# Four edits around the retention core and the down projections of a two-layer trunk: later residual rows, mixed items, own background buffers, output rows on ScalarE

## The chip, the cores and the metric

The kernel runs on one core of one Trainium2 chip. The metric is the device time of one execution in microseconds (us). Engines are named as in the profile: PE (TensorE matmul), PEld (its weight load), DVE (VectorE), ACT (ScalarE), POOL (GpSimd), SP (SyncE, which issues most DMAs).

## The reference

Two layers over a sequence of 1024 rows of width 1024, all in float32. Layer 0 mixes with a gated delta net, layer 1 with retention; each layer then has a convolutional feed-forward part. What the change touches is this:

```python
for i in range(DEPTH):
    mod = (e @ ada_w[i] + ada_b[i])[:, None, :]
    sh1, sc1, g1, sh2, sc2, g2 = jnp.split(mod, 6, axis=-1)
    y = mixers[i % N_MIXERS](x * (1.0 + sc1) + sh1)
    x = layer_norm(DN_ALPHA * x + (1.0 + g1) * y, ln_g[i, 0], ln_b[i, 0])
    y = conv_ffn(x * (1.0 + sc2) + sh2, ffn_up[i], ...)
    x = layer_norm(DN_ALPHA * x + (1.0 + g2) * y, ln_g[i, 1], ln_b[i, 1])

def retention(h, w_in, w_out):          # 4 heads, dk 256, dv 512, chunks of 128
    q, k, v, gate = split(h @ w_in)
    q, k = rot(q), rot(k) * dk ** -0.5  # rotary embedding
    # per head and chunk: state (256 x 512), scores (128 x 128) with a decay mask
    o = intra + inter                   # 128 x 512 for each head and chunk
    o = _standardize(o, 1e-6) * silu(gate)
    return o @ w_out
```

`_standardize` subtracts the mean and divides by the standard deviation of each row of 512.

## The kernel before

Float32 products are made of three products of split operands: `split` (L88) makes a high part with ACT (L89) and the rest with DVE or POOL (L90), and each pair is multiplied three times. The stages follow one another on the one core: the start and the gated delta net (to about 660 us in the profile), its output projection, the up projection of layer 0 (to 1195), its down projection (to 1430), retention's queries, keys and gates (to 1765), the retention core together with the value projection (to 2140), retention's output projection, then the up projection (2297 to 2740) and the down projection of layer 1.

**Order.** The program is unrolled in Python. A scheduler orders each engine's instructions by simulated times, and buffers belong to tags: `tl(tag, ...)` takes one of `BUFS[tag]` buffers, and a tile waits until the oldest one is free. In the delta net and in the core, `run` interleaves generators ("streams") by a planner's clock: a stream that yields a number comes back after so many planned us, and of those ready the one with the smallest priority goes first. The order of PE's matmuls there is fixed by `pq` (L642). The planned waits of the core are in `RL` (L1823): for instance `"b": 3.21` between the normalisation of a chunk's output and its transposes.

**Background work.** `bg` is a list of small units, and `bg_step` (L119) runs at fixed places: it finishes the pending unit and starts the next, so that a unit's data is loaded one step ahead. `bg_ada` makes the modulation vectors from `ada_w` (512 KB a unit, eight units a vector; L214 loads, L221 and L223 multiply and add on DVE). `bg_tag` names the buffers: "lane" within a Strassen stage, otherwise "wr", of which there are two and which also hold the raw weights of `load_w`. When head 2 of the core starts, `bg_ada(1, 2, "row")` adds eight units. `bg_gain` scales rows of the layer's input on POOL for later.

**Strassen stages.** `strassen` runs a list of items, each a pair of 128-column weight blocks, by seven products of half-size blocks (`wino`, L1216). The first two items go another way (`side`). PSUM results are copied by ACT (L1224), combined by DVE (L1154, L1213) and handed to the item's `sink`. In layer 1 the items are gates (`gate_item`: SiLU on ACT at L1667, then stored) and ropes (`rope_item`: for each half of the rows six DVE operations, L1651 to L1656, then stored; one item each for the query and key of a head). They come as two gates, eight ropes, six gates.

**Down projection.** `proj_gen` (L1274) makes seven products, p = 0 to 6, of `nj` = 11 steps each with `gate=None`: each step loads a left and a right block, splits them (`ops`, L1322), and does twelve matmuls. The results become the residual sum and the layer norm of two row halves (`finish`, `norm`). The residual of half 1 needs x scaled by the norm's gain and bias; `gain_half(n)` does this for 128 rows by 512 columns: load, two POOL operations (L1345), store from POOL's queue (L1346). It is called at steps 0, 2, 4 and 6 of p = 0 and 1. Half 0 is loaded at p = 2 and scaled on DVE (L1353), and half 1 is loaded at p = 5 (`xload`, L1348).

**Core.** For each head and chunk, `core` (L1728) makes the new state (`sc<-vv,kz`, two banks of tag `sc`, of which there are two), prepares the next chunk (`ret_front`: scores, transposed key `kz`), makes the output `po` in another `sc` bank (`sc<-vv,sThl` and, in float32, `sc<-Sr,qk`) and starts `ret_back`. That one takes the statistics from PSUM (L1774), normalises on DVE (L1780) into `on`, and after RL["b"] transposes `on` on PE (`mm<-cst,on`), multiplies by the gate (L1789) and stores the blocks, with four sums on POOL from chunk 4 on (L1811).

## Time and profile before

| what | value |
|---|---|
| median of 3 runs | 2973.52 us (2968.97 to 2977.79) |
| span of the profiled execution, first to last instruction | 2967.8 us |
| mean granted TensorE clock | 0.985 |
| PE / DVE / ACT / POOL busy, share of the span | 95% / 76% / 44% / 16% |
| DMA | 451.01 MB, mean 152 GB/s |

The profiled execution's own time is known by its span alone; the times of the runs hold some us more than a span, for what lies before the first and after the last instruction. Busy times are shares of the whole span, so a stage must be read by itself. Rows of the groups give line, engine, operation, output and inputs, count, then busy us and mean ns, then the idle time of the engine before them with what ended it. Rows of the waits give who waited for whom: us in total, times, longest. Rows of the stretches give start and end, length, busy us (count) of PE, PEld, DVE, ACT and POOL, the granted clock, the DMA share and GB/s. Rows of the timeline give start, length, engine, line and operation. Rows of one line's or one tile's instructions give minimum, median and maximum in ns.

### The profile page before, as it was taken

The numbers are of one execution on the slowest core, as the hardware profiler recorded it, in microseconds if no ns is written. First come the engines' busy times: TensorE is split into PE (matmuls) and PEld (weight loads), VectorE is DVE, ScalarE is ACT, GpSimd is POOL, SyncE is SP. The second block draws the span as 40 slices with busy tenths as digits, with TensorE's granted clock in tenths as the row PEclk, the third lists the DMA queues.
The fourth block names the chain that finished last, engine by engine and source line by source line (L and its number), as shares of the span: only waits on it lengthen the run. The fifth ranks groups of instructions, "written<-read, shape, count | busy, mean of one in ns | idle before, by whom it ended". The sixth has DMA issues, their size and how long they took to land. (4 is left out here: it accounts for less than half of the span.)

```text
span 2967.8 us, 38939 instructions
## 1 busy us (share of the span) xinstructions
PE 2820.5 (95%) x13638; PEld 2304.5 (78%) x13638; DVE 2242.4 (76%) x4005; ACT 1316.5 (44%) x2413; POOL 474.8 (16%) x469
## 2 busy tenths in 40 slices
PE   8999898999999999999999999999999999999997
PEld 7887777887788888787877887777777788887786
DVE  5787787656688888879678645666689887777979
ACT  4744564444544444446433442222344544444443
POOL 0312221100001111610000202322202011112301
PEclk9999999999999999999999999999999999999998
DMA  7231222254245445865333544665664243335753
GB/s 275 79 113 65 86 79 79 83 167 160 91 158 163 158 151 174 305 198 179 120 128 117 181 160 152 203 189 175 205 212 157 91 135 107 107 107 176 274 183 137
DMA packets 244404, 451.01 MB, mean 152 GB/s; under 512 B 23088, under 2 KB 76592, under 8 KB 244208
## 3 DMA queue, kind: packets, MB, share of 16 engines
q1 hardware_dynamic: 213088, 401.07, 41.0%
q10 hardware_dynamic: 29760, 43.00, 4.0%
q0 software_dynamic: 1360, 4.46, 0.4%
q8 instruction: 107, 1.75, 0.3%
q14 instruction: 89, 0.73, 0.1%
HBM read 339.91 MB, written 108.53 MB: 151 GB/s over the span
## 5 line engine op out<-in xcount | busy, mean ns | idle before, releaser
L651 PE MATMUL acc<-hT,wh 128*128 128x512 f32 x960 | 299.3, 393 | 0.0
L1437 PE MATMUL acc<-bb,ab 128*128 128x512 f32 x984 | 231.4, 393 | 6.6 <-DVE bb L90 5.4
L1585 POOL TENSOR_TENSOR o<-o 128x512 f32<-128x512 f32 x80 | 110.7, 1394 | 716.4 <-DVE o L1578 490.8
L1437 PEld LDWEIGHTS acc<-bb,ab 128*128 128x128 f32 x984 | 182.6, 188 | 50.2 <-DVE bb L90 10.2
L1163 PE MATMUL acc<-T,wb 128*128 128x512 f32 x840 | 203.1, 391 | 6.7 <-DVE wb L90 6.7
L651 PEld LDWEIGHTS acc<-hT,wh 128*128 128x128 f32 x960 | 181.9, 190 | 34.1
L651 PE MATMUL acc<-hT,wl 128*128 128x512 f32 x480 | 201.1, 419 | 0.0
L89 ACT ACTIVATE ab<-ar 128x512 fp32r<-128x512 f32 x210 | 129.6, 625 | 152.7 <-PE mm L287 36.9
L90 DVE TENSOR_TENSOR ab<-ar,ab 128x512 fp32r<-128x512 f32 x210 | 161.9, 777 | 41.1 <-ACT ab L89 41.1
L1163 PEld LDWEIGHTS acc<-T,wb 128*128 128x128 f32 x840 | 157.0, 188 | 43.2 <-DVE wb L90 9.8
L90 DVE TENSOR_TENSOR wl<-wr,wh 128x1024 fp32r<-128x1024 f32 x95 | 119.7, 1260 | 69.6 <-ACT wh L89 68.6
L90 DVE TENSOR_TENSOR wb<-mm,wb 128x512 fp32r<-128x512 f32 x216 | 145.5, 682 | 31.2 <-ACT wb L89 30.6
L90 DVE TENSOR_TENSOR wb<-wr,wb 128x512 fp32r<-128x512 f32 x162 | 111.1, 691 | 69.8 <-ACT wb L89 69.1
L89 ACT ACTIVATE wh<-wr 128x1024 fp32r<-128x1024 f32 x95 | 100.7, 1061 | 132.3 <-PE acc L651 53.1
L1224 ACT ACTIVATE pc<-acc 128x512 f32<-128x512 f32 x143 | 84.9, 593 | 160.7 <-PE acc L1163 97.4
L1564 DVE SCALAR_TENSOR_TENSOR o<-g,vc,o 128x512 f32<-128x512 f32 (+2 forms) x176 | 145.4, 843 | 4.7 <-ACT o L1559 4.1
L89 ACT ACTIVATE wb<-mm 128x512 fp32r<-128x512 f32 x216 | 124.0, 595 | 51.9 <-DVE mm L1213 50.3
L89 ACT ACTIVATE wb<-wr 128x512 fp32r<-128x512 f32 x162 | 99.4, 628 | 104.0 <-DMA wr<-in_ffn_up 38.8
L651 PE MATMUL acc<-wh,hT 128*128 128x512 f32 x384 | 135.6, 415 | 1.6 <-DVE vv L90 1.6
L110 PE MATMUL acc<-T,wb 128*128 128x512 f32 x292 | 116.0, 397 | 9.4 <-DVE wb L90 9.4
L472 DVE SCALAR_TENSOR_TENSOR qkv<-raw,vc,qkv 128x512 f32<-128x512 f32 x144 | 111.6, 779 | 11.5 <-ACT qkv L470 10.7
L223 DVE SCALAR_TENSOR_TENSOR ada<-mvw,e,ada 128x512 f32<-128x512 f32 x140 | 106.9, 764 | 17.4 <-DMA mvw<-in_ada_w 17.1
(641 smaller groups left out, 7466.8 us busy)
## 6 DMA issues: line engine op xcount, KB each, us to landing
wr<-in_ffn_up SPq DMA_DIRECT2D x92, 512.0 KB, 4.4
mvw<-in_ada_w SPq DMA_DIRECT2D x80, 512.0 KB, 4.3
ad<-o SPq DMA_DIRECT2D x154, 256.0 KB, 3.1
ar<-ad SPq DMA_DIRECT2D x154, 256.0 KB, 3.9
Br<-in_ffn_down SPq DMA_DIRECT2D x88, 256.0 KB, 3.8
wr<-in_ret_wv SPq DMA_DIRECT2D x32, 512.0 KB, 3.9
ar<-od SPq DMA_DIRECT2D x56, 256.0 KB, 5.3
xs<-xt ACTq DMA_DIRECT2D x24, 512.0 KB, 3.7
```

Of the source, the lines that this page charges most:

```text
L89: act.activation(dst_h, src, AF.Copy)
L90: eng.tensor_tensor(dst_l, src, dst_h, ALU.subtract)
L110: mm(acc, wl[:, k], hl[0], start=first, stop=False)
L223: dve.scalar_tensor_tensor(a, wr[:, kk], e[:, k:k + 1], a, ALU.mult, ALU.add)
L472: dve.scalar_tensor_tensor(oh, raw[:, 3 - j:515 - j], w[:, 3 - j:4 - j], oh, ALU.mult, ALU.add)
L651: pq(pe.matmul(out, lhsT, rhs, start=start, stop=stop), cost)
L1163: return pe.matmul(*a, skip_group_check=True, **kw)
L1224: act.activation(t, X, AF.Copy)
L1437: return pe.matmul(*args, skip_group_check=True, **kw)
L1564: dve.scalar_tensor_tensor(tv, gv[:, c0 - j:c1 - j], w[:, 2 - j:3 - j], tv, ALU.mult, ALU.add)
L1585: (dve if fp == 0 else pool).tensor_tensor(o[d], o[x], o[y], op)
```

## The change

- The row scaling of half 1 (`gain_half`) is called in p = 3 and 4 instead of p = 0 and 1, and its tile comes from the tag "xT" instead of "lane".
- The tag "xT" has two buffers instead of four; with the tiles that it now holds each is 4 KB a partition instead of 2.
- `bg_step` counts down: a unit returns a number of steps with its work. That is 2 where `bg_tag` is "xT", else 1. During the core `bg_tag` is "xT". The accumulator tile is taken when the work is done and not when the load is issued.
- After the first two gates, the order of items is rope, then three times rope and gate, rope, then three times rope and gate.
- `ret_back` copies `po` from PSUM with ACT, takes the statistics from the copy, makes minus mean times inverse deviation (one DVE and one POOL operation on a column) and normalises the copy in place with ACT (Identity with scale and bias). RL["b"] is 6.5 instead of 3.21.

```diff
-            "wr": 2, "wh": 2, "wl": 2, "t2": 3, "sm": 14, "sm2": 6, "st": 8, "s8": 6, "S": 4, "qx": 3, "fs": 1, "xT": 4}
+            "wr": 2, "wh": 2, "wl": 2, "t2": 3, "sm": 14, "sm2": 6, "st": 8, "s8": 6, "S": 4, "qx": 3, "fs": 1, "xT": 2}
...
     def bg_step(tile=mm_tile):
         bg_ps[0] = tile
-        if pend:
-            pend.pop()()
+        for p in pend:
+            p[0] -= 1
+        while pend and (pend[0][0] <= 0 or not bg):
+            pend.pop(0)[1]()
+            if not bg:
+                break
         if bg:
             nxt = bg.pop(0)()
             if nxt:
-                pend.append(nxt)
+                pend.append(list(nxt))
...
         def unit(nh, kp):
+            wr = tl(bg_tag[0], [P, 2, HALF], name="mvw")
+            c0 = j * D + nh * HALF
+            sp.dma_start(wr, A["ada_w"][i, kp * 256:(kp + 1) * 256, c0:c0 + HALF].rearrange("(a p) n -> p a n", p=P))
+            return 2 if bg_tag[0] == "xT" else 1, lambda: work(nh, kp, wr)
+
+        def work(nh, kp, wr):
             if kp == 0:
                 box["a"] = tl("ada", [P, HALF])
             a = box["a"]
...
-            x = tl("lane", [P, HALF], name="xg")
+            x = tl("xT", [P, HALF], name="xg")
...
-                if gain and p < 2 and j % 2 == 0 and p * 4 + j // 2 < 8 and j < 8:
-                    gain_half(p * 4 + j // 2)
+                if gain and p in (3, 4) and j % 2 == 0 and j < 8:
+                    gain_half((p - 3) * 4 + j // 2)
...
-    B = strassen(h0, xts, sc_r, sh_r, [gate_item(0), gate_item(2)]
-                 + [rope_item(h, j) for h in range(RH) for j in range(2)] + [gate_item(u) for u in range(4, 16, 2)], ("hTa", "aux", "qkv", "qkv", "hTa"), True)
+    ropes = [rope_item(h, j) for h in range(RH) for j in range(2)]
+    gates_ = [gate_item(u) for u in range(4, 16, 2)]
+    mixed = [ropes.pop(0)] + [r for k in range(3) for r in (ropes.pop(0), gates_.pop(0))] + [ropes.pop(0)]
+    mixed += [r for k in range(3) for r in (ropes.pop(0), gates_.pop(0))]
+    B = strassen(h0, xts, sc_r, sh_r, [gate_item(0), gate_item(2)] + mixed, ("hTa", "aux", "qkv", "qkv", "hTa"), True)
...
     def ret_back(h, n, po):
+        on = tl("t2", [P, HALF], name="on")
+        act.activation(on, po, AF.Copy)
         st = tl("st", [P, 2, 6], name="rst")
-        dve.bn_stats(st[:, 0], po)
+        dve.bn_stats(st[:, 0], on)
         mv = tl("s8", [P, 4], name="mv")
         dve.bn_aggr(mv[:, 0:2], st[:, 0])
         dve.tensor_scalar(mv[:, 2:3], mv[:, 1:2], 1e-6, None, ALU.add)
+        dve.tensor_scalar(mv[:, 1:2], mv[:, 0:1], -1.0, None, ALU.mult)
         pool.tensor_tensor(mv[:, 3:4], mv[:, 2:3], mhalf[:, 0:1], ALU.pow)
-        on = tl("t2", [P, HALF], name="on")
-        dve.tensor_scalar(on, po, mv[:, 0:1], mv[:, 3:4], ALU.subtract, ALU.mult)
+        pool.tensor_tensor(mv[:, 0:1], mv[:, 1:2], mv[:, 3:4], ALU.mult)
+        act.activation(on, on, AF.Identity, bias=mv[:, 0:1], scale=mv[:, 3:4])
         yield RL["b"]
...
-    RL = {"v": 2.57, "q": 5.9, "f": 3.35, "p": 0.55, "c": 2.75, "b": 3.21, "o": 4.42}
+    RL = {"v": 2.57, "q": 5.9, "f": 3.35, "p": 0.55, "c": 2.75, "b": 6.5, "o": 4.42}
...
+    bg_tag[0] = "xT"
     run([(0.0, ret_fill())] + [(-1.0, core(h)) for h in range(RH)])
+    bg_tag[0] = "wr"
```

More of the change, by code (lines that the diff above doesn't have):

```diff
@@ L211, in unit @@
             a = box["a"]
-            wr = tl(bg_tag[0], [P, 2, HALF], name="mvw")
-            c0 = j * D + nh * HALF
-            sp.dma_start(wr, A["ada_w"][i, kp * 256:(kp + 1) * 256, c0:c0 + HALF].rearrange("(a p) n -> p a n", p=P))
-            return lambda: work(nh, kp, a, wr)
-        def work(nh, kp, a, wr):
             for kk in range(2):
@@ L389, in unit @@
                 return gain(x, rs, c)
-            return lambda: gain(x, rs, c)
+            return 1, lambda: gain(x, rs, c)
         def gain(x, rs, c):
```

## The prediction

> **What bounds the kernel now.** I read the page first, then the busy time of the engines in stretches that follow the stages, then the waits of PE in each stage, and last the timeline at single waits.
>
> ```profile
> span 2967.8 us, 38939 instructions
> PE 2820.5 (95%) x13638; PEld 2304.5 (78%) x13638; DVE 2242.4 (76%) x4005; ACT 1316.5 (44%) x2413; POOL 474.8 (16%) x469
> ```
>
> PE is the bound almost everywhere, so the change can win only the time in which PE stands still, 147 us at most, and of that only what lies in the stages that it touches. Those are the two down projections (1196 to 1430 and 2736 to 2968), the Strassen stage of the retention's q, k and gates (about 1481 to 1765) and the retention core (1765 to 2140).
>
> ```profile
> core 0: us, PE busy (x) PEld busy (x) DVE busy (x) ACT busy (x) POOL busy (x), PEclk, DMA share, GB/s
> 1196.00:1236.00 40.00, 33.00 (x137) 25.89 (x136) 33.83 (x40) 18.12 (x39) 31.98 (x18) 0.96 1.02 376
> 1236.00:1265.00 29.00, 29.00 (x129) 24.01 (x128) 28.98 (x39) 15.85 (x28) 21.29 (x9) 1.00 0.79 272
> 1326.00:1356.00 30.00, 30.00 (x134) 24.83 (x133) 24.65 (x41) 8.49 (x15) 0.00 (x0) 1.00 0.46 148
> 1356.00:1394.00 38.00, 36.18 (x168) 28.75 (x167) 36.46 (x71) 26.90 (x45) 3.60 (x4) 1.00 0.59 194
> 1765.00:2140.00 375.00, 350.97 (x1568) 269.45 (x1567) 232.24 (x419) 93.61 (x159) 96.67 (x113) 0.99 0.59 182
> 2829.00:2859.00 30.00, 30.00 (x134) 24.83 (x133) 18.84 (x30) 13.14 (x24) 0.00 (x0) 1.00 0.61 194
> 2859.00:2890.00 31.00, 31.00 (x139) 25.66 (x137) 30.63 (x52) 13.44 (x25) 0.00 (x0) 1.00 0.59 187
> 2890.00:2919.00 29.00, 29.00 (x129) 24.02 (x128) 29.00 (x56) 16.43 (x31) 4.37 (x3) 1.00 0.49 155
> 2919.00:2949.00 30.00, 29.51 (x128) 23.49 (x126) 26.80 (x51) 7.19 (x12) 5.43 (x3) 1.00 0.39 132
> ```
>
> A down projection is seven products of eleven steps, about 30 us each. The first two rows are products p = 0 and 1 of layer 0, rows three and four its p = 4 and 5; the last four rows are p = 3 to 6 of layer 1. Three things are to be seen. At the start (1196) PE misses 7 us of 40 while POOL is busy for 32 and the DMA engines are full. In the core PE misses 24 us of 375, and ACT is idle for three quarters. And in the last layer DVE has 11.2 us free in p = 3, but is full from 2859 on: there DVE, not PE, sets when the kernel ends.
>
> The waits of PE, by stage: 1196 to 1236, 2720 to 2800, 1481 to 1765, and the core.
>
> ```profile
> PE acc L285 <- DVE ab L90: 7.0, 4, 2.8
> ...
> PE acc L285 <- DVE ab L90: 4.9, 3, 2.6
> PE acc L286 <- DVE bb L90: 0.8, 2, 0.4
> ...
> PE acc L1163 <- DVE wb L90: 5.3, 5, 1.1
> PE sc L1163 <- DVE wb L90: 2.7, 3, 1.1
> ...
> PE sc L651 <- DVE on L1780: 8.0, 6, 2.5
> PE mm L654 <- DVE on L1780: 7.2, 4, 3.1
> PE sc L651 <- DVE Sr L1752: 3.5, 1, 3.5
> ...
> PE acc L651 <- DVE wl L90: 1.0, 2, 0.8
> ```
>
> These 40 us are all that can be reached: 12.7 at the starts of the two down projections, 8.0 in the Strassen stage, 19.7 in the core.
>
> **Later residual rows.** Eight times a layer, `gain_half` loads 256 KB, runs two POOL operations on it and stores it from POOL's queue. This leaves p = 0 and 1 and goes to p = 3 and 4, four in each. What POOL does to DVE is seen in the splits of the left operand, in 1196 to 1265 (first row) and in 2859 to 2965, where POOL hardly works (second); the third row is one POOL operation.
>
> ```profile
> L90 DVE TENSOR_TENSOR ab<-ar,ab 128x512 fp32r<-128x512 f32 x26 | 26.0, 1014 | 7.6 <-ACT ab L89 7.6
> ...
> L90 DVE TENSOR_TENSOR ab<-ar,ab 128x512 fp32r<-128x512 f32 x29 | 19.5, 677 | 0.0
> ...
> L1345 POOL TENSOR_TENSOR xg<-xg,rowb x32: 1257/1625/20702, 1199.6 to 2782.6; 128x512 f32<-128x512 f32 x32
> ```
>
> Beside POOL the split takes 1014 ns instead of 677: 26 x 0.337 = 8.8 us of DVE in that stretch from this group alone, with 27 POOL instructions beside it. At the start, where no operands are ahead yet, PE waits for just these splits. The four sums of the last feature pair (L1585) stay on POOL, and the first operands still have to land, so I let 2.0 of the 7.0 us stay in layer 0 and 1.7 of 5.7 in layer 1: -5.0 and -4.0.
>
> What it costs later: p = 3 hides its four rows (11.2 us of free DVE in layer 1; layer 0 runs the same products). In p = 4 there are eight POOL operations and four stores. Their price to DVE lies between 8.8 / 27 x 12 = 3.9 us and the full length of the operations, 8 x 1.257 = 10.1; I take 6, since the splits are only the largest of DVE's groups. In layer 0, p = 4 leaves DVE 5.35 us free and the next product 1.5, so 0.5 is left over. In layer 1 nothing covers it, and DVE's chain to the end grows: +6. DVE works in order, so the splits for the next steps and the residual sums of p = 4 queue behind a held operation, and PE waits for the splits. SP's queue gains the loads in p = 3 and 4 where the DMA share is 0.46 to 0.61, which I count as nothing; on a full queue, as at 1196, they would delay operand loads. The rows are read only in the half-1 loads of p = 5. Layer 0: -4.5 (-7 to +3). Layer 1: +2 (-5.7 to +6.1).
>
> The Trainium skill, SBUF — State Buffer (section "SBUF: two separate sides"), says that VectorE and GpSimd share one port pair as an exclusive lock: whichever starts first holds it for its whole instruction, and the other fully blocks. The longer splits agree in kind; by the whole-instruction price the upper end, 10.1, would hold, which speaks against the move into a full DVE.
>
> **The core's output rows.** In `ret_back` DVE reads `po` from PSUM, and its last reader is the normalisation (L1780), which waits for POOL's power (L1778). Groups of the core, one small DVE operation, and the nearest row to the new normalisation (ACT, Identity with bias and scale columns):
>
> ```profile
> L651 PE MATMUL sc<-Sr,qk 128*128 128x512 f32 x112 | 52.6, 592 | 0.0
> ...
> L1780 DVE TENSOR_SCALAR on<-sc,mv 128x512 f32<-128x512 f32 x32 | 25.9, 808 | 34.6 <-POOL mv L1778 34.6
> ...
> L89 ACT ACTIVATE vv<-acc 128x512 fp32r<-128x512 f32 x32 | 19.1, 596 | 37.3 <-PE acc L651 33.8 <-DVE mv L1777 2.4
> L1778 POOL TENSOR_TENSOR mv<-mv,mhalf 128x1 f32<-128x1 f32 x32 | 17.6, 551 | 135.0 <-DVE mv L1777 135.0
> ...
> L1811 POOL TENSOR_TENSOR ot<-ot,op 128x256 f32<-128x256 f32 x15 | 14.5, 967 | 1.9 <-DMA od<-ot 1.8
> ...
> 1898.86 0.15 DVE L1777 TENSOR_SCALAR mv<-mv 128x1 f32<-128x1 f32 x1
> ...
> L1376 ACT ACTIVATE xt<-xt,mv x8: 802/810/817, 2919.5 to 2961.8; 128x512 f32<-128x512 f32 x8
> ```
>
> After the change PSUM is free after one ACT copy, 0.6 us by the `vv` row, which waits for no POOL. The six waits of PE for the `sc` bank, 8.0 us, go. What is late next is the bank's own turn:
>
> ```profile
> 1894.42 0.47 ACT L1719 ACTIVATE kz<-mm,vc 128x256 fp32r<-128x256 f32 x1 [3.63 <-PE mm L654]
> ...
> 1892.70 0.50 PE L651 MATMUL sc<-vv,kz 128*128 128x512 f32 x1 [1.02 <-DVE on L1780]
> ...
> 1901.15 1.07 PE L651 MATMUL sc<-vv,kz 128*128 128x512 f32 x4
> ```
>
> A chunk's state matmuls (`sc<-vv,kz`) need `kz`, which ACT begins at 1894.42 and PE uses at 1901.15, 6.7 us later, so ACT can be late by some 5 us at no cost.
>
> The chain to the transposes of `on` grows: copy 0.60, negation 0.15, POOL product 0.55, with the normalisation equal (0.81 on both engines): +1.3 us. The planner's delay b goes from 3.21 to 6.5, which puts the transposes behind the next chunk's `po`, whose four state matmuls alone take 52.6 / 28 = 1.9 us. The slack grows by at least 0.6, so of the 7.2 us (four waits) I take off 3. Bounds: all of it, or 4 x 1.3 = 5.2 more. DVE loses 32 x 0.81 = 26 us of work and the 34.6 us in which it stood before L1780 with `Sr`, `kz` and `wl` queued behind; it isn't the bound here, so this counts nothing. ACT gains 32 x 1.41 = 45 us in a stage where it is idle for 281, and takes over the wait for POOL, with `kz`, `sThl`, `wh` and `vv` behind it. I charge 2 us for that (0 to the price of the third rival). Together -8 - 3 + 2 = -9.
>
> **Own background buffers.** The eight loads of `ada_w` in the core share the two `wr` buffers with the value weights, and DVE stands in order before their data:
>
> ```profile
> DVE ada L223 <- DMA mvw<-in_ada_w: 12.0, 5, 4.9
> ```
>
> With two `xT` buffers and a countdown of two steps, each work item comes a step later than now, and a step is about one chunk, 9 us, against the 4.9 waited at most. PE's two waits behind it (`Sr` 3.5, `wl` 1.0) should go: -4 (-4.5 to 0). SP issues the same loads. With a count of 1, as everywhere else, `bg_step` does what it did; at the start only two `xT` tiles are used.
>
> **Mixed items.** Each rope item adds twelve DVE operations, and PE waits once an item, 8.0 us over eight waits. The first row is in a rope item, the second in the first gate item after the last rope, as the ACT row (SiLU of a gate) shows:
>
> ```profile
> 1549.50 0.72 PE L1163 MATMUL acc<-T,wb 128*128 128x512 f32 x2 [1.06 <-DVE wb L90]
> ...
> 1651.51 0.73 PE L1163 MATMUL acc<-T,wb 128*128 128x512 f32 x2 [1.06 <-DVE wb L90]
> ...
> 1651.07 0.61 ACT L1667 ACTIVATE pc<-pc 128x512 f32<-128x512 f32 x1
> ```
>
> The wait is the same, 1.06 us. It belongs to the item that follows a rope, whatever that is: the rope's operations run into it. There are still eight such items, so I take 0 (-8.0 if the gates drain them, +4 if output DMAs and `cv` buffers of two kinds collide).
>
> **The sum.** -4.5 + 2 - 9 - 4 + 0 = -15.5 us. Against the profiled span that is 2952.3. The median of the runs, 2973.5, lies 5.7 above the span, launch and spread together; I carry that over: 2958.
>
> **The rivals.** First, mixing drains the burst: without the eight waits it is 2950. For it: DVE is less loaded in gate items; against it: the two rows above.
>
> Second, POOL holds DVE for the whole length of its operations: 10.1 instead of 6 in p = 4 of both layers. Layer 0 then has 10.1 - 5.35 = 4.7 left over instead of 0.5, layer 1 gets 10.1: +8.3, 2966. For it: DVE is at 100% from 2859; against it: POOL's 20.7 us maximum shows that DVE also holds off POOL. The Trainium skill's page SBUF — State Buffer, cited above, would give this one.
>
> Third, slower: ACT stands before the new normalisation until POOL has worked off its queue. POOL's sums (up to 1 us each, four together) and the remaining row gains already made DVE wait 34.6 us in 26 waits. It decides when ACT is late by more than the 5 us at `kz`, or the transposes by more than their 0.6 us. If then each of 32 chunks costs PE 1.5 us, as the ten waits of now do on average (15.2 / 10), that is 48 instead of 15.2: +33 and the other terms' -6.5, 3000. Against it: ACT's idle 75%.
>
> Fourth, nothing comes of the core: the released bank is not what PE needs, and the next wait (for `Sr` or a split) takes the place of the 11 us. Then 2969.
>
> **How the numbers follow.** The forecast has 0.50, with a range of its own of 2948 to 2966; mixing 0.13; the full hold 0.12; ACT 0.12; the core for nothing 0.13. A measurement here can tell about 0.3%, 8.9 us: faster is below 2964.6. That holds for most of the forecast (0.47), the mixing (0.13), and some of the full hold and the core (0.09): 0.69. The same: 0.03 + 0.16 = 0.19. Slower: 0.12. The range of 2938 to 2980 holds all but the third rival and the lower bounds of several terms at once.
>
> **What would show it.** Right: no PE wait on `on` for `sc` in the core, under 5 us for its transposes; no DVE wait for `mvw`; PE waits under 4.5 us at the starts of the down projections; rope waits of about 1.06, eight times; DVE's work after PE's last matmul some us longer. Wrong: ACT waiting for POOL with `kz` late; the last layer's p = 4 to 6 longer by over 8 us; no more waits after ropes.

## The result and the profile after

The changed kernel takes 2975.4 us (median of 20 runs, 2963.6 to 2983.4), the kernel before 2973.7 (20 runs): ratio 1.0004, 95% interval 0.9995 to 1.0014. Nothing that can be measured came of it. The time is inside the range of the prediction, but not the gain of 15.5 us. The profiled execution has 3.3 us more span than that of before. First the page of the changed kernel:

```profile
span 2971.1 us, 39084 instructions
...
PE 2821.3 (95%) x13638; PEld 2306.7 (78%) x13638; DVE 2220.4 (75%) x4005; ACT 1360.0 (46%) x2477; POOL 479.4 (16%) x501
```

PE does as many matmuls as before, so the two traces can be laid side by side by the time at which the k-th matmul begins. The difference, after minus before, at the edges of the stages, worked out from both traces (one execution of each kernel):

| from matmul to matmul (about, us) | difference goes from, to | change | forecast |
|---|---|---|---|
| start of layer 0's down projection (1145 to 1268) | -2.8 to -12.2 | -9.4 | -5 |
| its p = 2 to 6 (to 1496) | -12.2 to +6.7 | +18.9 | +0.5 |
| q, k and gates (to 1734) | +6.7 to +2.9 | -3.8 | 0 |
| passage into the core (to 1791) | +2.9 to +10.4 | +7.5 | none |
| core (to 2213) | +10.4 to +9.3 | -1.1 | -13 |
| layer 1's down projection (2568 to its last matmul, 2949) | +9.5 to +3.7 | -5.8 | +2 |

The rows moved from the start are worth more than forecast, in both layers. One place takes that back at once: p = 3 and 4 of layer 0. The stretches of the changed kernel, columns as in the prediction:

```profile
1196.00:1236.00 40.00, 40.00 (x179) 33.11 (x178) 31.96 (x52) 24.31 (x51) 20.14 (x4) 1.00 0.85 304
...
1326.00:1356.00 30.00, 23.25 (x96) 19.12 (x97) 26.42 (x44) 5.14 (x9) 0.00 (x0) 0.83 0.55 180
...
1765.00:2140.00 375.00, 355.46 (x1563) 272.57 (x1564) 205.14 (x407) 133.04 (x220) 108.58 (x145) 0.97 0.59 183
...
2859.00:2890.00 31.00, 30.11 (x133) 24.95 (x134) 30.28 (x51) 12.23 (x23) 0.00 (x0) 1.00 0.61 187
```

In the first row PE is busy for all of its 40 us, against 33.00 before. In the second it does 96 matmuls where 134 were done before, at a granted clock of 0.83: it stood, and then ran slowly for a while. The core does as many matmuls in 375 us as before (1563 against 1568), although DVE works 27 us less in it.

The waits of PE in the changed kernel, for 1310 to 1345, 1481 to 1750, 1750 to 1800 and the core:

```profile
PE sc L289 <- DVE u L1414: 16.5, 1, 16.5
...
PE acc L1167 <- DVE wb L90: 3.9, 5, 1.1
PE sc L1167 <- DVE wb L90: 1.6, 2, 1.0
...
PE acc L655 <- DVE vv L90: 1.7, 2, 0.9
PE acc L655 <- ACT wh L89: 1.1, 1, 1.1
PE mm L270 <- DMA xlo<-xs: 1.1, 1, 1.1
...
PE mm L658 <- ACT on L1790: 9.3, 4, 4.4
PE acc L655 <- DVE ab L90: 3.8, 1, 3.8
PE acc L655 <- DVE vv L90: 3.0, 5, 0.9
```

One wait of 16.5 us is new. The waits after ropes fell from 8.0 to 5.5, but at 1750 to 1800 `xlo`, `wh` and `wl` are waited for as well, where before there was one wait of 1.0 for `vv`. In the core the waits of `sc` on the output row are gone, as forecast, and those of its transposes are 9.3 instead of 7.2.

**The wait of 16.5 us, followed back.** DVE stood first; then what SP's queue did (waits of SP from 1270 to 1335, then its timeline):

```profile
DVE Br L1321 <- DMA Br<-in_ffn_down: 18.1, 3, 16.3
```

```profile
SPq L1347 <- DMA xg<-xg: 24.6, 4, 10.9
SPq L1636 <- POOL xg L1349: 7.7, 3, 4.2
...
SPq L215 <- DMA xg<-xg: 2.5, 2, 1.4
```

```profile
1309.17 0.44 SPq L1307 DMA_DIRECT2D Br<-in_ffn_down  x1
...
1317.07 0.33 SPq L1636 DMA_DIRECT2D trig<-in_trig  x1
1318.84 0.38 SPq L215 DMA_DIRECT2D mvw<-in_ada_w  x1
1319.32 0.42 SPq L1307 DMA_DIRECT2D Br<-in_ffn_down  x1
```

SP issues one load after the other. The load of a row (L1347) waits until one of the two `xT` buffers is free, that is until the store of the row two back has landed; the loads of the rotary tables (L1636) wait for buffers that the rows' gain and bias hold; the core's first background units (L215), which the scheduler has moved up to here, wait for the same two buffers. Behind all of them stand the operand loads. The block `Br` that DVE needs was issued at 1319.32 and DVE went on at 1324.49. PE's wait ends at 1332.75, at the first matmul of p = 4.

The rows were late for a reason of their own. POOL's first scaling, and DVE beside it:

```profile
1259.17 13.92 POOL L1349 TENSOR_TENSOR xg<-xg,rowb 128x512 f32<-128x512 f32 x2 [33.73 <-DMA xg<-xs]
...
1269.56 0.69 DVE L90 TENSOR_TENSOR ab<-ar,ab 128x512 fp32r<-128x512 f32 x1
1270.76 1.18 DVE L90 TENSOR_TENSOR ab<-ar,ab 128x512 fp32r<-128x512 f32 x1 [0.52 <-ACT ab L89]
1271.87 1.77 DVE L90 TENSOR_TENSOR bb<-Bw,bb 128x512 fp32r<-128x512 f32 x1
```

```profile
L1349 POOL TENSOR_TENSOR xg<-xg,rowb x16: 1262/1453/12222, 1259.2 to 1317.1; 128x512 f32<-128x512 f32 x16
```

The last row (minimum, median and maximum in ns) shows one of the first two operations at 12.2 us against a median of 1.45. DVE worked without a gap at 0.69 us an operation, and only after its first gap (0.52 us at 1270) did POOL come through and DVE's operations grow to 1.2 to 2.5 us. The two longest scalings of the kernel before (20.7 and 13.1 us) end the same way: all three are done some 1.15 us after DVE's first gap since their start begins.

The rows don't run where the prediction placed them either. They are called in the steps of p = 3 and 4, but operands are made about a product ahead of PE: in layer 0 POOL scales from 1259 to 1318, while PE is in p = 2 and 3 (from 1256 up to its wait), and in layer 1 from 2799 to 2852, again in p = 2 and 3 (2799 to 2860):

```profile
L1349 POOL TENSOR_TENSOR xg<-xg,rowb x16: 1286/1622/2487, 2799.1 to 2850.1; 128x512 f32<-128x512 f32 x16
```

### The profile page after: what moved, and what is told of

The parts are those of the page before. It is cut to its first block, busy times and chain, and to the rows that moved or that the text cites. A ratio compares the mean times of both kernels' runs of the same rounds, so it can differ in the third digit from the quotient of the medians.

```text
span 2971.1 us, 39084 instructions
## 1 busy us (share of the span) xinstructions
PE 2821.3 (95%) x13638; PEld 2306.7 (78%) x13638; DVE 2220.4 (75%) x4005; ACT 1360.0 (46%) x2477; POOL 479.4 (16%) x501
## 4 chain that ended last, share of the span: by engine, by line
PE 74%; DVE 11%; DMA 6%; ACT 5%; issue 3%; POOL 1%; SPq 0%; ACTq 0%; POOLq 0%; DVEq 0%
PE acc L655 15%; PE acc L1167 10%; PE acc L110 6%; PE acc L111 5%; PE acc L112 5%; PE sc L1167 5%; PE sc L655 4%; PE acc L1441 3%; PE mm L655 2%; PE sc L111 2%; PE sc L112 2%; PE sc L110 2%; DVE ab L90 1%; PE mm L658 1%; DVE bb L90 1%
## 5 line engine op out<-in xcount | busy, mean ns | idle before, releaser
L1589 POOL TENSOR_TENSOR o<-o 128x512 f32<-128x512 f32 x80 | 126.8, 1595 | 792.0 <-DVE o L1582 558.8
L1167 PE MATMUL acc<-T,wb 128*128 128x512 f32 x840 | 203.0, 390 | 5.0 <-DVE wb L90 5.0
L110 PE MATMUL acc<-T,wb 128*128 128x512 f32 x292 | 116.0, 397 | 9.4 <-DVE wb L90 9.4
L111 PE MATMUL acc<-T,wb 128*128 128x512 f32 x292 | 115.5, 396 | 0.0
```

Source lines behind the costliest of these rows:

```text
L110: mm(acc, wl[:, k], hl[0], start=first, stop=False)
L111: mm(acc, wh[:, k], hl[1], start=False, stop=False)
L1167: return pe.matmul(*a, skip_group_check=True, **kw)
L1589: (dve if fp == 0 else pool).tensor_tensor(o[d], o[x], o[y], op)
```

## The experiments

Times are medians; a ratio is to the kernel before, run on the same chip, with its 95% interval. The versions are named in bold. "C" is the changed kernel.

### The rows and SP's queue

**Rows back.** C with

```diff
-            x = tl("xT", [P, HALF], name="xg")
+            x = tl("lane", [P, HALF], name="xg")
...
-                if gain and p in (3, 4) and j % 2 == 0 and j < 8:
-                    gain_half((p - 3) * 4 + j // 2)
+                if gain and p < 2 and j % 2 == 0 and p * 4 + j // 2 < 8 and j < 8:
+                    gain_half(p * 4 + j // 2)
```

> The changed kernel with the row scaling back at steps 0 to 6 of p = 0 and 1, in the buffers of the lane; the rest stays changed. Theory (the row loads wait for buffers on SP's queue, and the operand loads of layer 0's p = 3 and 4 stand behind them): PE's single wait of 16.6 us for u is gone, and the starts of the two down projections lose their gains of 9.5 and 8.8 us again. Against the changed kernel -19.6 + 9.5 + 8.8 - 2.7 = -4 us, about 2971. Rival (the long wait comes from elsewhere, the other loads that were hoisted into p = 4): the 16.6 us stay and the starts are lost as well, 2993.

2973.3 us, 1.0004 (0.9993 to 1.0015). PE has no wait at all from 1270 to 1345. So the late rows bring the long wait, and as C has them they are worth nothing that can be told; the theory's -4 is within the uncertainty, the rival's 2993 is not.

**Rows from POOL's queue.** C with

```diff
             with after("w"):
-                sp.dma_start(x, gain[1][rs, hs(hf)])
+                pool.dma_start(x, gain[1][rs, hs(hf)])
```

> The changed kernel, with the eight row loads of each layer issued from POOL's queue instead of SP's; the POOL work and the place stay. Theory: the 24.6 us in which SP stood before row loads are gone, but four loads of the rotary tables stand in SP's queue ahead of the operand loads of p = 3 and wait for the buffers of the row vectors, which are held until the last row is done; so SP stands there once, for 5 to 20 us, and PE's wait in p = 3 or 4 falls only in part, to 5 to 12 us: 2965 to 2972. Rival (POOL takes DVE's port, and what is late is DVE's split): POOL does the same work and more issues, so the wait of 16.6 us stays, 2975.

2970.4 us, 0.9987 (0.9977 to 0.9996), and no wait of PE from 1270 to 1345. But this run doesn't answer its question: without SP's order to hold them, the scheduler moved the row loads to the start of the up projection (the units' loads of SP then stood 18.5 us there in the next version, and both lost nearly 8 us between the 4000th and the 5000th matmul, with one PE wait of 9.3 us for `wb` in the next version, 4.7 in C).

**The same, tables last.** Also

```diff
-                    sp.dma_start(t[hf], (A["trig"][i] if j else A["trigq"][h, i])[:, hs(hf)])
+                    with after("a"):
+                        sp.dma_start(t[hf], (A["trig"][i] if j else A["trigq"][h, i])[:, hs(hf)])
```

> As the one before, and the loads of the rotary tables are ordered behind the last left block of the down projection, so that no load of SP's queue waits for the row work. Theory: PE's wait in p = 3 and 4 is under 2 us, the loss of 19.6 us of that stretch is at most 3, against the changed kernel -16 to -19: 2957 to 2960, 0.5% below the kernel before. Rival (port): 16.6 us stay, 2975.

2967.9 us, 0.9983 (0.9973 to 0.9992). Against the kernel before, the profile stands at -4.1 after p = 1 and at -3.2 after p = 6: p = 2 to 6 cost 0.9 instead of 18.9. The total missed 2957 to 2960, since the place at the up projection cost nearly 8.

**Four buffers.** C with four buffers of 2 KB:

```diff
-            ... "fs": 1, "xT": 2}
+            ... "fs": 1, "xT": 4}
...
-    bg_tag[0] = "xT"
     run([(0.0, ret_fill())] + [(-1.0, core(h)) for h in range(RH)])
```

> The changed kernel with four buffers of 2 KB for the rows and the background units of the core back in the raw weights' buffers. Theory: each row's load waits for the store four rows back instead of two, so SP stands for under 8 us instead of 24.6, and the rotary tables' 7.7 us stay; PE's wait falls from 16.6 to 3 to 8 us, -9 to -14, and the core gets back DVE's wait for its unit (about +4 on PE, as before) but loses the 4.5 us stall of the transposes at 2044: 2961 to 2967. Rival (port): 2975.

2965.2 us, 0.9970 (0.9959 to 0.9982). The waits for row buffers are gone; what is left are the tables, as expected (PE, then SP):

```profile
PE sc L289 <- DVE u L1414: 6.6, 1, 6.6
```

```profile
SPq L1636 <- POOL xg L1349: 18.5, 4, 11.8
```

**Four buffers, tables last.** Both edits.

> The changed kernel with four row buffers of 2 KB, the core's background units back in the raw weights' buffers, and the rotary tables' loads ordered behind the last left block of the down projection: with the row loads still on SP, no load there waits for the row work for longer than the rows' own buffers make it. Theory (SP's queue): the 18.5 us in which SP stood for the tables in the version with four buffers alone are gone, PE's wait for u in layer 0's p = 4 (6.6 us there, 16.6 in the changed kernel) falls under 1.5, and the stretch p = 3 and 4 loses at most 2 us against the kernel before: -7 to -9 us against that version, 2956 to 2958. Rival (POOL and DVE share a port, the rest of 6.6 us is DVE's): as the version with four buffers, 2965.

2961.1 us, 0.9963 (0.9951 to 0.9975). No wait for row work is left in SP's queue, none on `u` in PE's; from matmul 6500 to 7500 the difference goes from -9.7 to -8.5. That settles it: POOL does the same row work in the same products, and without SP's waits the stretch costs 1.2 us. (POOL's first scaling took 8.6 us in this trace. In "Late rows and own buffers" below it took 12.3, as in C, and PE has no wait on `u` there either.) The price of the queue by itself is this version against C without own buffers (below, 2976.4 on the same chip, the same rows in two buffers): 15 us.

### One part of C undone

**Items as before.** C with

```diff
-    B = strassen(h0, xts, sc_r, sh_r, [gate_item(0), gate_item(2)] + mixed, ...
+    B = strassen(h0, xts, sc_r, sh_r, [gate_item(0), gate_item(2)]
+                 + [rope_item(h, j) for h in range(RH) for j in range(2)] + [gate_item(u) for u in range(4, 16, 2)], ...
```

> The changed kernel with the items in the order of before (two gates, eight ropes, six gates). Theory (mixing wins 3.5 us of waits after ropes and loses 7.5 us where the stage goes over into the core, since the last rope ends at 1747 instead of 1652 us and its stores, the loads of q and k and the first row scalings then fall on the first value weights): the loads of xlo land before they are needed again, no PE waits over 0.9 us from 1755 to 1800, and -4 us against the changed kernel, to -7 if the transposes' wait of 3.4 us at 1879 goes as well: 2968 to 2971. Rival (the loss at the stage's end belongs to the core's edit): the rope waits return and nothing else moves, +3.5, 2979.

2970.8 us, 0.9991 (0.9981 to 1.0001), 0.13% or 4 us better than C's 1.0004, as the theory has it, though the intervals overlap. In the profile the waits after ropes are back (5.8 and 3.2), the passage into the core costs 0.1 us instead of 7.5, and at 1750 to 1800 there is only this:

```profile
PE acc L655 <- DVE vv L90: 1.0, 1, 1.0
```

**Output rows on DVE as before.** C with the whole head of `ret_back`, and b, of before:

```diff
-        act.activation(on, po, AF.Copy)
-        dve.bn_stats(st[:, 0], on)
+        dve.bn_stats(st[:, 0], po)
...
-        pool.tensor_tensor(mv[:, 0:1], mv[:, 1:2], mv[:, 3:4], ALU.mult)
-        act.activation(on, on, AF.Identity, bias=mv[:, 0:1], scale=mv[:, 3:4])
+        dve.tensor_scalar(on, po, mv[:, 0:1], mv[:, 3:4], ALU.subtract, ALU.mult)
```

> The changed kernel with the output rows of the core on DVE as before, with the delay b of 3.21. Theory (the 8.0 us of PE waits for sc are gone, the transposes' waits grow from 7.2 to 10.0, and what is gained is lost again to the slower clock after stalls of 3 to 5 us): without the edit the sc waits return, about +5 us against the changed kernel, 2980. Rival (core for nothing): within 2 us of the changed kernel, 2973 to 2977; a slower clock for some matmuls follows every long wait in both.

2964.3 us, 0.9972 (0.9960 to 0.9984): by the ratios 9.5 us faster than C, where the forecast's gain of 9 and my expectation both had it slower. Both theories fall. In the core the trace gains 10 us on C. It also waits less in the down projection, 6.7 us on `u` instead of 16.5 with the same order of loads: POOL's first scaling took 8.7 us here and 12.2 in C. In the two other versions with these two row buffers the scaling took 12.3 us, and PE waited 16.9 us ("Items as before") and 16.5 (the next version). So the runs' 9.5 us can't be divided between the two; the core's edit by itself follows on clean ground.

**Background units in the raw weights' buffers again.** C with

```diff
-    bg_tag[0] = "xT"
     run([(0.0, ret_fill())] + [(-1.0, core(h)) for h in range(RH)])
```

> The changed kernel with the core's background units back in the raw weights' buffers (the two 4 KB buffers hold rows only). Theory: the units' loads no longer stand in SP's queue behind the rows in layer 0's p = 4 (2.5 us less of the 16.6), and the transposes' wait of 4.5 us at 2044, where DVE stood before a unit whose load was issued at 2031, is gone; DVE's waits for units come back in the core, with 4.0 (vv), 2.0 (kz) and 2.3 us (Sr) on PE as in the version with four buffers: between -3 and +3, 2972 to 2978. Rival (own buffers are worth the forecast 4 us): +4, 2979.

2976.4 us, 1.0009 (0.9996 to 1.0021): no difference from C that can be told.

### The parts on clean ground

**Own buffers alone.** The kernel before with nothing but the two 4 KB buffers, the countdown and

```diff
+    bg_tag[0] = "xT"
     run([(0.0, ret_fill())] + [(-1.0, core(h)) for h in range(RH)])
+    bg_tag[0] = "wr"
```

> The kernel before with one part of the change: two 4 KB buffers of their own and the countdown of two steps for the core's background units; rows, items and output rows as before. Forecast of the prediction: -4 us (the Sr and wl waits of PE behind DVE's unit waits go), 2968. Rival, from the trace of the changed kernel without the core's edit (which is 10.1 us ahead of the kernel before from the start of the core's first chunks to its end): the units' loads shared their two buffers with the value weights and held those too, -8 to -10, 2962 to 2964.

2959.5 us, 0.9950 (0.9934 to 0.9967): -12 us, three times the forecast of this part, and more than the rival. PE's waits on the output row in the core, then DVE's wait for the units, then the units' products (minimum, median and maximum in ns, first and last start):

```profile
PE mm L658 <- DVE on L1784: 5.6, 4, 2.9
...
PE sc L655 <- DVE on L1784: 2.3, 3, 1.7
```

```profile
DVE ada L227 <- DMA mvw<-in_ada_w: 0.7, 1, 0.7
```

```profile
L227 DVE SCALAR_TENSOR_TENSOR ada<-mvw,e,ada x14: 742/745/1298, 1486.3 to 2020.9; 128x512 f32<-128x512 f32 x14
```

The same products in the kernel before:

```profile
L223 DVE SCALAR_TENSOR_TENSOR ada<-mvw,e,ada x14: 730/750/1230, 1934.3 to 2027.0; 128x512 f32<-128x512 f32 x14
```

They began at 1934, and now begin at 1486. With buffers that nobody else uses, the scheduler places half of the units ahead of the core. DVE's wait goes from 12.0 to 0.7, and with it go PE's waits for `Sr` and `wl` (in the kernel before, 3.5 us at 1975, when DVE had stood 4.4 for a unit at 1972). Against the kernel before, the trace gains 8.3 us from 1964 to 2027. Whether the buffers or the two steps of countdown do it was not separated.

The waits of `sc` on the output row fall as well, 8.0 to 2.3, but not for one reason. Three of the six in the kernel before (1834, 1845 and 1893, together 4.2 us) come before the first unit is loaded at 1929. There DVE waits for POOL's power, which stands behind row scalings:

```profile
1840.95 1.30 POOL L393 TENSOR_TENSOR xg<-xg,gb 128x512 f32<-128x512 f32 x1 [7.79 <-DMA xg<-xs]
1842.32 1.28 POOL L394 TENSOR_TENSOR xg<-xg,gb 128x512 f32<-128x512 f32 x1
1843.56 0.55 POOL L1778 TENSOR_TENSOR mv<-mv,mhalf 128x1 f32<-128x1 f32 x1
...
1844.15 0.81 DVE L1780 TENSOR_SCALAR on<-sc,mv 128x512 f32<-128x512 f32 x1 [3.78 <-POOL mv L1778]
```

In the version with own buffers, scaling and power fall a little differently, and these places cost 0.6 us. The other three (3.8 us, 1938 to 2032) lie where units are in DVE's queue; before the last, 2.5 us, DVE again waits for POOL, which is at its sums. Of these 1.7 stay.

**Late rows and own buffers.** Rows in turn from two tags, tables and units behind the last left block, items and output rows as before:

```diff
-            x = tl("xT", [P, HALF], name="xg")
+            x = tl(("xT", "t2")[n % 2], [P, HALF], name="xg")
...
+            with after("a"):
                 sp.dma_start(wr, A["ada_w"]...   # and the same for the tables
```

> Late rows without any load of SP that waits long for them (row buffers in turn from two tags, five in all; the loads of the rotary tables and of the core's units ordered behind the last left block of the down projection), own buffers for the core's units, items and output rows as before. Theory (the terms add up): -9.7 us at the start of layer 0's down projection with nothing lost in p = 3 and 4, -8.7 + 2.5 in layer 1, -8 to -10 in the core: -24 +- 3 against the kernel before, 2946 to 2951. Rival (what one wait gives, the next takes: the core's own buffers win only beside the mixed order): -14, 2958.

2940.4 us, 0.9891 (0.9873 to 0.9908): 31 us faster than before and the fastest complete version. The late rows, with the loads ordered so that none waits long, are worth 19 us here (against own buffers alone, same chip), where the prediction had -2.5 for both layers. The two traces agree on the place: this one gains 9.5 us in layer 0's down projection and 8.5 in layer 1's. The ordering of the tables and units alone was not run. Its profiled execution is the slowest of its five.

**The same with output rows on ScalarE**, that is the diff of "Output rows on DVE as before" the other way, with b of 6.5.

> As the one before (late rows that hold no load, own buffers, order of items of before), with the change's output rows on ScalarE and b of 6.5. Theory (the normalisation on ACT stands behind POOL's queue and DVE's unit waits, and the transposes on PE behind it, whatever else is in the kernel): +8 to +10 us against that one, all of it in the core, with two or more waits of over 3 us on ACT's row; 2957. Rival (the edit costs only beside the mixed order, which pushes the first six row scalings of POOL to 1738 to 1780): within 2 us of that one or faster by up to the 8 us of sc waits.

2953.5 us, 0.9932 (0.9916 to 0.9949): +13 us, 0.41%, intervals apart. The waits of PE for the transposes without the edit and with it, then ACT's wait with it:

```profile
PE mm L659 <- DVE on L1786: 6.6, 4, 3.4
...
PE sc L656 <- DVE on L1786: 1.9, 2, 1.1
```

```profile
PE mm L659 <- ACT on L1789: 9.3, 4, 4.4
...
ACT on L1789 <- POOL mv L1788: 44.9, 18, 5.0
```

The edit can only win 1.9 us of `sc` waits here; it loses 2.7 at the transposes, and ACT stands 45 us for POOL. These waits alone come to 1 us, not 13. The pair of traces, of which the one without the edit is its slowest, differs by 5 us, and 6.2 are lost in one place: the wait of 4.4 us at 2026 and the slow matmuls behind it (granted clock 0.90 from 2000 to 2030, 1.00 without the edit). At 2016 to 2019 DVE had stood 3.3 us for a unit's load there, with the row's statistics behind it.

**The same with ACT's copy only**, without the edit of the one above:

```diff
+        act.activation(on, po, AF.Copy)
-        dve.bn_stats(st[:, 0], po)
+        dve.bn_stats(st[:, 0], on)
...
-        dve.tensor_scalar(on, po, mv[:, 0:1], mv[:, 3:4], ALU.subtract, ALU.mult)
+        dve.tensor_scalar(on, on, mv[:, 0:1], mv[:, 3:4], ALU.subtract, ALU.mult)
```

> As the version with late rows that hold no load, own buffers and the order of items of before, and of the core's edit only the first step: ACT copies the output row out of PSUM, the statistics are taken from the copy, and DVE normalises the copy (b stays 3.21). Theory (the gain is the released bank, the price is the normalisation on ACT): PE's waits on the row for sc (8.0 us before) are under 1, the transposes' wait grows by at most 4 x 0.6, so -3 to -6 us against the version without it. Rival (the bank is worth nothing, as the next wait takes its place): within 2 us of it. Second rival (the longer chain costs what it does on ACT): +5 or more.

2955.9 us, 0.9938 (0.9922 to 0.9954): +15.5 us; the second rival. The transposes' wait is 19.0 us in seven times, 7.6 the longest. What stood ahead in POOL's queue then, while DVE waited for L1786 from 1858.7:

```profile
1857.57 1.70 POOL L1818 TENSOR_TENSOR ot<-ot 128x256 f32<-128x256 f32 x1
1859.23 1.26 POOL L398 TENSOR_TENSOR xg<-xg,gb 128x512 f32<-128x512 f32 x1
1860.45 1.26 POOL L399 TENSOR_TENSOR xg<-xg,gb 128x512 f32<-128x512 f32 x1
1861.67 0.72 POOL L1818 TENSOR_TENSOR op<-ot,op 128x256 f32<-128x256 f32 x1
1862.35 0.55 POOL L1786 TENSOR_TENSOR mv<-mv,mhalf 128x1 f32<-128x1 f32 x1
```

The copy makes the statistics later, and at this place the step that comes to POOL a little later falls behind whole row scalings and sums.

**Without POOL's row scalings**, the output rows on DVE and on ScalarE. In `bg_gain`:

```diff
         def gain(x, rs, c):
-            pool.tensor_tensor(x, x, gb[0], ALU.mult)
-            pool.tensor_tensor(x, x, gb[1], ALU.add)
             sp.dma_start(dst[rs, hs(c)], x)
```

> The version with late rows that hold no load, own buffers, and items and output rows as before, without POOL's scaling of the sixteen row blocks beside the core (32 operations of 1.3 us are left out, so the residual that layer 1 reads is unscaled; loads and stores stay). Theory (POOL works in order, and the inverse deviation of an output row stands behind the scalings): the transposes' wait of 3.4 us falls under 1, DVE's 26 us of waits for POOL fall by half, -4 us against 2940: 2936. Rival (the chain itself is late): 2940.

> The same left out of the version that also has the output rows on ScalarE with b of 6.5 (2953 with the scalings). Theory (POOL's queue): ACT's waits for POOL's product, 44.9 us in 18 waits, fall under 15, PE's waits for the normalised row from 9.3 to under 4, and the edit costs at most 4 us more than DVE's normalisation does without the scalings: 2936 to 2941. Rival (the chain over ACT and POOL and the later transposes cost by themselves): ACT's waits stay near 45 us or PE finds others, +10 or more against that one: 2946 to 2952. The wait of 4.6 us at 2026 behind DVE's unit stays in both.

2937.2 us, 0.9876 (0.9861 to 0.9891), and 2947.0 us, 0.9911 (0.9896 to 0.9927). In both traces 5 to 6 us are won at about 1860, but the edit still costs 10 us: the theory of POOL's queue covers a part at most. ACT still waits 41.0 us for POOL's product, so most of that wait is not the scalings'. PE's longest wait of the version on ScalarE is 4.3 us at 2021. There DVE stood 3.2 us for a unit's load, with the row's statistics behind it.

**Scalings on DVE.** "Late rows and own buffers" with `dve.tensor_tensor` for the two operations of `gain`.

> The version with late rows that hold no load, own buffers, and items and output rows as before, with the sixteen row blocks beside the core scaled on DVE instead of POOL. Theory (POOL's queue): as without the scalings, less what 20 operations of 0.7 us in the core add to DVE, which is idle there for a third: -3, 2937. Rival (DVE's queue is what PE waits for): +3 to +8, 2943 to 2948.

2950.3 us, 0.9920 (0.9903 to 0.9937): the rival's side, and 2 us past it; 13 us above the version without the scalings on the same chip. PE's longest wait for the transposes is 4.5 against 3.4. The trace shows no such loss in one place, so how the rest comes about stays open.

**Mixed items on clean ground.** "Late rows and own buffers" with `mixed` as in C.

> The version with late rows that hold no load, own buffers, and output rows as before, with the change's mixed order of items. Theory (mixing wins some 4 us of waits after ropes and loses 7 at the end of its stage and 3 in the core, where the first row scalings and q and k come later): +5 to +7, 2945 to 2947. Rival (the loss at the stage's end came from the loads held in layer 0's down projection): -4, 2936.

2946.8 us, 0.9909 (0.9894 to 0.9924): 5 us above the version without mixing by the ratios, which were taken on two chips and whose intervals overlap, so that mixing costs anything is not shown. Against the trace without mixing it gains 8.5 us from matmul 7500 to 8250 and has given 8.2 of them back by matmul 8750 (the core's first chunks). So the rival falls: with no load held in layer 0, the loss at the stage's end is still there.

**Units ahead of the core**, with DVE's and with ScalarE's rows:

```diff
-        if h == 2:
-            bg_ada(1, 2, "row")
...
+    bg_tag[0] = "xT"
+    bg_ada(1, 2, "row")
+    while bg or pend:
+        bg_step()
     bg_gain(1, xs[1], xg[0])
```

> The version with late rows that hold no load, own buffers, and items and output rows as before (2940), with the last modulation row's units issued ahead of the core instead of at head 2, so that no unit's work stands in DVE's queue inside the core. Theory (the units are what DVE stands for): the wait for sc of 1.3 at 2015 goes, otherwise little: 2936 to 2940. Rival (the units' work on DVE moves to the stage before the core or its start and costs there): +2 to +4.

> The same with the output rows on ScalarE (2953 with the units in the core). Theory (DVE's unit with the statistics behind it makes the stall of 4.5 us at 2021 to 2026 and the slow matmuls after it): no transposes' wait over 3.5 us after 1900, and the edit costs at most 6 us against the version of this pair without it: 2940 to 2946. Rival (the chain itself, DVE to POOL to ACT, and the transposes placed later by b): the stall stays or turns up elsewhere, and the edit costs 9 to 13 us: 2947 to 2952.

2943.7 us, 0.9909 (0.9889 to 0.9929), and 2948.5 us, 0.9925 (0.9909 to 0.9942). With no unit in the core the edit costs 4.8 us instead of 13, and the transposes' wait at 2022 is 1.1 us instead of 4.4; the intervals overlap, so whether any cost is left can't be told. The units' place itself won nothing, the rival's side for the version on DVE. With no unit in the core, PE waits 3.7 us for `sc` at 1826 and 1837, where POOL's power again stands behind row scalings.

## Why the prediction was wrong, step by step

**What failed: "SP's queue gains the loads ... which I count as nothing".** The prediction weighed the queue by the share of busy DMA engines (0.46 to 0.61), which says nothing of a load that may not be issued. The change gives the rows two buffers instead of four, and the prediction did not ask what stands behind a load that waits for one. That cost 16.5 us of PE at once, 18.9 in the stretch where +0.5 was forecast, and about 15 by the pair of runs. The row loads and the tables were two causes in one queue, with the hoisted units (2.5 us of SP) as a third, and undoing one only showed the next (16.5, 6.6, none).

That the time still fell inside the range is luck. Against their forecasts the stages are off by +18.4 (p = 2 to 6), +11.9 (core) and +7.5 (passage) one way and by -4.4 (start), -3.8 (items) and -7.8 (layer 1) the other.

**The starts were right in kind, too small in size.** They gave -9.4 and, in layer 1, -8.8 from 2568 to 2803 (9.5 to 0.7), against -5 and -4. I counted PE's waits and left a part of them standing; none was left, and the slower matmuls that follow a wait went as well. The granted clock of 1196 to 1236 is 1.00 in the changed kernel and was 0.96.

**POOL against DVE was priced in the wrong place.** I charged DVE with 6 us in p = 4 of layer 1, where it is full from 2859 on. The rows were done by 2852. They ran in p = 2 and 3, where DVE had been free for 7.8 and 11.2 us. The second figure is in the prediction, the first is from this row of the kernel before (29.00 less 21.25):

```profile
2800.00:2829.00 29.00, 29.00 (x129) 24.02 (x128) 21.25 (x36) 13.99 (x25) 0.00 (x0) 1.00 0.50 154
```

From 2803 to the last matmul layer 1 lost 3.0 us, and layer 0 lost 1.2 without the queue. In layer 0 POOL was the one held longest, 13.9 us for two operations, and its lateness went on to SP through the buffers. The sum for layer 0 has a slip as well: 6 less 5.35 leaves 0.65 and not 0.5.

The Trainium skill, SBUF — State Buffer (section "SBUF: two separate sides"), has an exclusive lock for one whole instruction. A wait for one DVE instruction would be 0.7 us here; the trace shows POOL out for some 11 us of back-to-back DVE instructions, so the measured length is far above what one held instruction explains. The second rival's price, 10.1 us in layer 1, did not come, but since the rows missed the full DVE, neither its rule nor my 6 us was put to the test there.

**The core's terms were not independent.** I summed -8 (`sc` bank), -3 (transposes), +2 (ACT) and -4 (own buffers). With own buffers alone 6 of the 8 went and the `Sr` and `wl` waits, -12 in all. The waits named "DVE on" looked like a wait for the bank; behind 4.2 of the 8.0 us stood POOL's row scalings, and the rest came where units were on DVE, most of it with POOL late as well. What remained for ScalarE to win was 2 us, and it cost 13, or 5 that can't be told from nothing where no unit stands in the core. One cause is shown: where a unit's load stops DVE ahead of the row's statistics, the transposes wait 4.4 us, and 1.1 without a unit there. No run leaves out both the units and the scalings, so what else it costs stays open. The fourth rival ("the core for nothing") is nearest for C: the core changed by 1.1 us. The third had the mechanism, ACT standing for POOL (45.8 us in 18 waits in C), but not the price: PE waited 9.3 us for the output rows, not 48, and the slack at `kz` held: no wait of PE for `kz` is in the core's list.

**"Each work item comes a step later than now"** was wrong too: half of the units' work came some 450 us earlier, as the traces with own buffers show (1486 instead of 1934). In C this put two of their loads into SP's queue at 1318.

**Mixed items** were forecast at 0. The waits fell by a third (first rival), -3.8, and the ropes that now end at 1753 instead of 1653 push their stores, the loads of q and k and six row scalings into the passage to the core: +7.5. The prediction looked at the stage alone and did not ask what follows it. Without mixing the passage costs 0.1 us, so the 7.5 are the mixing's.

**What held.** The `sc` waits on the output row went, the starts run without a wait, the items come in the order described. The end of the kernel did not grow: 18.7 us lie between PE's last matmul and the last instruction before, 18.4 after.

## What to carry to other kernels

Before moving a load in an in-order queue, list what each load there waits for and which loads stand behind it; a buffer count that is halved can be a wait in that queue, whatever the DMA engines' share says. Look up when an operation really runs: one that is called in a step can run a product earlier. Follow each wait to its first cause before giving it to an edit: six waits under one name had two causes here, and the edit that was to remove them all was left with 2 us. A part that loses in a bundle is not a bad part: here two of four gave 31 us without the other two, once their loads were ordered.

## What was not expected of the hardware

POOL can be kept out by DVE for far longer than one operation lasts: 12.2 us for a 128x512 scaling with a median of 1.45, ended by DVE's first gap of 0.5 us, and 20.7 us in the kernel before, ended by a gap of 0.4.

A stall of PE costs more than its length. Its timeline in the changed kernel after the wait of 16.5 us:

```profile
1332.75 0.77 PE L289 MATMUL sc<-bb,ab 128*128 128x512 f32 x1 [16.45 <-DVE u L1414]
1333.32 0.63 PE L290 MATMUL sc<-bb,ab 128*128 128x512 f32 x1
...
1335.45 0.63 PE L289 MATMUL sc<-bb,ab 128*128 128x512 f32 x1
...
1336.15 0.39 PE L291 MATMUL sc<-bb,ab 128*128 128x512 f32 x1
```

Six matmuls take 0.63 us each before the 0.39 of the steady state comes back, 0.2 us lost on each start.
